# Block inverse of a gated-DeltaNet encoder: third 32x32 form in turn with the second, fifth 64x64 form in turn with the fourth of the next group

## The chip, the cores and the metric

The kernel runs on one core of one Trainium2 chip. The metric is device time of one execution in microseconds (us), lower is better. A core has a matrix engine (PE, TensorE, with weight loads listed apart as PEld), a vector engine (DVE), an activation engine (ACT), a general engine (POOL) and a queue engine for transfers (SP); each works through its own list of instructions in order, and they wait for each other by semaphores.

## What is computed

The reference is a two-layer encoder: in each layer a combined projection feeds a bidirectional chunked gated-delta-rule group (4 heads of 128) and a short gated convolution, then an output projection, then a SwiGLU feed-forward. The part that matters here is the triangular solve within each chunk, cut to its core:

```python
M = jnp.where(strict, jnp.einsum('bnhid,bnhjd->bnhij', kb, k) * decay_mat, 0.0)
A = M + jnp.eye(CHUNK, dtype=M.dtype)
u = lax.linalg.triangular_solve(A, vb, left_side=True, lower=True, unit_diagonal=True)
w = lax.linalg.triangular_solve(A, kb * jnp.exp(G)[..., None], left_side=True, lower=True,
                                unit_diagonal=True)
```

Instead of solving, the kernel forms the inverse of A once for each chunk, head and direction and multiplies by it in the scan over chunks. It uses chunks of 128 positions and a first chunk of 16.

## The kernel before

Data lie with channels on the 128 partitions and positions along the free dimension. A layer runs: input projection (function `dense`, lines 157 to 159, three matrix products for each part of the contraction, because each operand is split into a high and a low part), convolutions and gates, the chunk matrices and their inverses, the scan (`scan_step`), the output projection and the feed-forward. The dense products are TensorE's steady stream; all the rest is placed between them. After each stretch of a dense product has been recorded, `dense` takes one function from each of the lists `jobs`, `jobs2` and `jobs3` and calls it. `low(f)` records the matrix products of `f` at the place in the priority order that the dense products have reached, so that the scheduler, which orders the instructions of each engine by priority and by its own estimate of when they are ready, puts them among the dense ones.

The inverse of a 128x128 unit triangular block is built from its diagonal 32x32 blocks up. There are 32 such blocks (8 chunks x 4 heads) for each direction `d` in each layer, so four inverses in all. First DVE inverts the 32x32 diagonal blocks by substitution (`substitute`, lines 523 and 525), two 32x32-transposes (lines 534 and 535) give them in both orientations, and ACT writes one of them into the big matrix `P_` (line 537). Then `invert(d)` returns seven functions, which `jobs3` hands out one at a time:

- `first` (line 550): for each of 32 blocks q and two pairs (f, s) of neighbouring 32-strips, the product of the off-diagonal block with one diagonal inverse. ACT moves it to `QS` with its sign changed (line 553).
- `second` (line 558): `QS` of strip s times the other inverse, for the two pairs in turn; ACT moves it into `P_` (line 561). This gives the 64x64 inverses.
- `third` (line 568): the same product transposed, for the first pair only; ACT moves it into `X64` (line 569), and DVE fills the rest of `X64` with copies and zeros (lines 570 to 572).
- `fourth(qh)` and `fifth(qh)` (lines 579 and 584): the two 64x64 products that join the 64x64 inverses into 128x128 ones, for a group of eight blocks (qh 0 to 3). The fourth reads partitions F_ and writes partitions S_, the fifth reads S_ and writes F_ (F_ and S_ are the two halves of 64 partitions, which half is which depends on `d`). ACT moves the fourth's result into `X64` (line 580), which is the fifth's operand, and the fifth's into `P_` (line 585).

Each form takes PSUM from `fb(c)`, one bank of 128 partitions x 512 words; there are two banks for each direction ("f" for d = 0, "b" for d = 1). The first three forms take one bank for each half of 16 blocks, the last two one for each group of eight. A form that has been handed out in one job is followed by some 17 to 24 dense or other products before the next. The last four jobs are two groups of the fourth, two of the fifth, and once more:

```python
return [first, second, third] + [lambda f=f, q=q: [f(q), f(q + 1)] for q in (0, 2) for f in (fourth, fifth)]
```

[...]

Of the kernel before, what the change touches and what calls it, by code (L numbers as in the profile page):

```python
# [10 lines left out]
AF = mybir.ActivationFunctionType  # L11
# [31 lines left out]
def trunk(ctx: ExitStack, tc: tile.TileContext, xT, w_in, w_ba, w_out, w_gu, w_dn,  # L43
          par_d, alog_d, dtb_d, cst_d, eye_d, out):
    nc = tc.nc
# [10 lines left out]
    def big(tag, dt=F32):  # L56
        return sb.tile([128, 4, L], dt, tag=tag, name=nm(tag))
# [10 lines left out]
    def bank(tag):  # L68
        return psp.tile([128, 512], F32, tag=tag, bufs={"acc": 3, "a": 1, "f": 2, "b": 2}[tag], name=nm("p" + tag))
# [4 lines left out]
    turn = [0]  # L74
# [20 lines left out]
    def at_prio(p):  # L95
        tc.cur_priority = p

    mm = nc.tensor.matmul
    act = nc.scalar.activation
# [180 lines left out]
    for l in range(DEPTH):  # L280
# [213 lines left out]
        B = [slice(32 * b, 32 * b + 32) for b in range(4)]  # L494
# [32 lines left out]
        def invert(d):  # L527
            P_ = Pv[d]
            W, Xi = subs[d]
            tmp = tmp0[0] if d == 0 else big(Y[0][2])  # L530
            XB = tmp[:, 3, 0:1024].rearrange("p (q c) -> p q c", q=32)

            ZB = W.rearrange("p a b -> p (a b)").rearrange("p (q i) -> p q i", q=32)
            nc.vector.transpose(out=XB.rearrange("p q c -> p c q"), in_=Xi.rearrange("p i c -> p c i"))
            nc.vector.transpose(out=ZB.rearrange("p q i -> p i q"), in_=Xi)
            for b in range(4):
                act(out=P_[B[b], :, B[b]], in_=ZB[B[b]], func=AF.Copy)
            pairs = [(0, 1), (2, 3)] if d == 0 else [(3, 2), (1, 0)]
            QS = tmp[:, 2, 0:1024].rearrange("p (q c) -> p q c", q=32)
            X64 = tmp[:, 0:2, :].rearrange("p a b -> p (a b)")[:, 0:2048].rearrange("p (q c) -> p q c", q=32)  # L540
            halves = [slice(0, 16), slice(16, 32)]

            def fb(c):
                return bank("fb"[d]).rearrange("p (q c) -> p q c", c=c)


            def first():
                for qs in halves:
                    ps = fb(32)
                    low(lambda: [mm(ps[B[s], q - qs.start, :], P_[B[f], q, B[s]], XB[B[f], q, :], start=True, stop=True, skip_group_check=True)  # L550
                                 for q in range(qs.start, qs.stop) for (f, s) in pairs])
                    for (f, s) in pairs:
                        act(out=QS[B[s], qs, :], in_=ps[B[s]], func=AF.Copy, scale=-1.0)

            def second():
                for qs in halves:
                    ps = fb(32)
                    low(lambda: [mm(ps[B[f], q - qs.start, :], QS[B[s], q, :], P_[B[s], q, B[s]], start=True, stop=True, skip_group_check=True)
                                 for q in range(qs.start, qs.stop) for (f, s) in pairs])
                    for (f, s) in pairs:  # L560
                        act(out=P_[B[f], qs, B[s]], in_=ps[B[f]], func=AF.Copy)

            def third():
                f, s = pairs[0]
                fo, so = 32 * (f % 2), 32 * (s % 2)
                for qs in halves:
                    ps = fb(32)
                    low(lambda: [mm(ps[B[s], q - qs.start, :], P_[B[s], q, B[s]], QS[B[s], q, :], start=True, stop=True) for q in range(qs.start, qs.stop)])
                    act(out=X64[B[s], qs, fo:fo + 32], in_=ps[B[s]], func=AF.Copy)
                    nc.vector.tensor_copy(X64[B[f], qs, fo:fo + 32], XB[B[f], qs, :])  # L570
                    nc.vector.tensor_copy(X64[B[s], qs, so:so + 32], XB[B[s], qs, :])
                    nc.vector.memset(X64[B[f], qs, so:so + 32], 0.0)


            F_, S_ = (slice(0, 64), slice(64, 128)) if d == 0 else (slice(64, 128), slice(0, 64))

            def fourth(qh):
                ps = fb(64)
                low(lambda: [mm(ps[S_, q, :], P_[F_, 8 * qh + q, S_], X64[F_, 8 * qh + q, :], start=True, stop=True) for q in range(8)])
                act(out=X64[S_, 8 * qh:8 * qh + 8, :], in_=ps[S_], func=AF.Copy, scale=-1.0)  # L580

            def fifth(qh):
                ps = fb(64)
                low(lambda: [mm(ps[F_, q, :], X64[S_, 8 * qh + q, :], P_[S_, 8 * qh + q, S_], start=True, stop=True) for q in range(8)])
                act(out=P_[F_, 8 * qh:8 * qh + 8, S_], in_=ps[F_], func=AF.Copy)

            return [first, second, third] + [lambda f=f, q=q: [f(q), f(q + 1)] for q in (0, 2) for f in (fourth, fifth)]

        l2s = {}

# [84 lines left out]
        def low(f):  # L675

            here = tc.cur_priority
            at_prio(mmp[0])
            f()
            mmp[0] = tc.cur_priority  # L680
            at_prio(here)
# [21 lines left out]
        for i in range(4):  # L703
            t = trow()
            if i == 3:
                jobs3.extend(invert(0))
            inproj(8 + i, to_row(t))
            v = trow() if i % 2 == 0 else row(Y[1] + "f")
            conv(t, v, P_CV + 3 * (8 + i))
            act(out=v, in_=v, func=AF.Silu)  # L710
            jobs.extend([lambda i=i, v=v, c0=c0: v_store(i, v, c0) for c0 in (0, 1, 5)])
# [25 lines left out]
        for j, q in enumerate((4, 5, 0, 6, 7, 1, 2, 3)):  # L737
            lov[0] = j < 2
            if j == 1:
                jobs2.extend([lambda c=c: chunk_a(c) for c in ca])  # L740
            if j == 3:
                jobs3.extend(invert(1))
            if q < 4:
                y3 = sc_tile(q)
            else:
                z_tile(q - 4)
            if j == 0:
                substitute(1)
# [531 lines left out]
        for f in range(FT):  # L1280
# [22 lines left out]
            ps = {}  # L1303
# [107 lines left out]
        for u, (p, b, m) in enumerate(UNITS):  # L1411
            if b == 1 and p in FIRST:
                dh, z = FIRST[p]
                q = 4 * dh + m
# [13 lines left out]
            for j in range(NJ):  # L1428
                ps = bks[m, j]
# [21 lines left out]
        else:  # L1451
# [22 lines left out]
            for (n0, n1) in FIN:  # L1474
                e = (n1 - n0) // 4
                sv = ss[:, n0:n1]
                ps = bank("a")
# [100 lines left out]
```

## Time and profile before

| | |
|---|---|
| median of 3 runs (lowest to highest) | 2513.88 us (2511.24 to 2517.37) |
| the profiled execution's own time | 2517.22 us |
| its span, first to last instruction | 2515.4 us |
| mean granted TensorE clock | 0.997 |
| DVE, ACT busy, share of the span | 67%, 42% |

The profile is one execution. Its span is what its views divide up; the 1.8 us between span and time lie before the first and behind the last instruction. A matrix product of 32-bit operands is two records in the trace, each with its own weight load, so counts of records are twice those of the code; the records overlap, since the next one starts before the last has drained, and so the start-to-start distance, not the length of a record, is what a product takes from the queue.

### The profile page before, as it was taken

To read this page: it belongs to the slowest core of one execution; us is meant where nothing else is said; L and a number is where in the kernel's file an instruction comes from. 1 tells how busy PE (TensorE), PEld (TensorE's weight loads), DVE (VectorE), ACT (ScalarE), POOL (GpSimd) and SP (SyncE) were. 2 spreads that over 40 slices of the span, in tenths; PEclk is the share of its full clock that TensorE was granted. 3 is DMA by queue.
4 is the path that set the end of the run, shared out by engine and by line. 5 is a ranking of instruction groups with operands and counts; after the bars stand their busy time and mean duration, and the time that the engine had idled before them with its cause. 6 is when DMAs were issued, how large, how long until landed. Compare 5 with 4: busy or idle time off the path is not lost. (4 is left out here: it accounts for less than half of the span.)

```text
span 2515.4 us, 44862 instructions
## 1 busy us (share of the span) xinstructions
PE 2478.2 (99%) x17508; PEld 2276.9 (91%) x17508; DVE 1696.9 (67%) x3073; ACT 1045.9 (42%) x1944; POOL 340.0 (14%) x359
## 2 busy tenths in 40 slices
PE   8999999999999999999999999999999999999998
PEld 6989999999999999999999888998977888887887
DVE  4788333649877777877657893336698777677765
ACT  5554333535333333344445543335453333234444
POOL 1031212331000000000111212133400000000012
PEclk9999999999999999999999999999999999999999
DMA  3444353624323332764224443446332233238541
GB/s 127 135 166 149 112 161 130 212 77 136 116 102 102 108 102 81 256 198 133 92 77 145 152 154 116 143 131 205 120 126 101 97 105 117 90 112 279 177 120 68
DMA packets 199530, 335.27 MB, mean 133 GB/s; under 512 B 23404, under 2 KB 85668, under 8 KB 199316
## 3 DMA queue, kind: packets, MB, share of 16 engines
q1 hardware_dynamic: 171204, 293.84, 35.3%
q10 hardware_dynamic: 25936, 34.19, 4.2%
q0 software_dynamic: 2176, 4.36, 0.6%
q8 instruction: 138, 2.26, 0.4%
q14 instruction: 76, 0.62, 0.1%
HBM read 250.31 MB, written 81.99 MB: 132 GB/s over the span
## 5 line engine op out<-in xcount | busy, mean ns | idle before, releaser
L131 POOL TENSOR_TENSOR wlo<-raw,whi 128x512 fp32r<-128x512 f32 x132 | 176.4, 1338 | 1285.4 <-ACT whi L130 1116.7
L157 PE MATMUL pacc<-a,whi 128*128 128x346 f32 (+1 forms) x808 | 263.6, 329 | 8.8 <-ACT whi L130 7.6
L159 PE MATMUL pacc<-a,wlo 128*128 128x346 f32 (+1 forms) x808 | 262.4, 326 | 0.7 <-DVE wlo L131 0.5
L157 PE MATMUL pacc<-b,whi 128*128 128x346 f32 (+2 forms) x672 | 234.0, 349 | 2.4 <-ACT b L900 1.8
L159 PE MATMUL pacc<-b,wlo 128*128 128x346 f32 (+2 forms) x672 | 233.1, 348 | 0.8 <-DVE wlo L131 0.8
L158 PE MATMUL pacc<-a,whi 128*128 128x346 f32 (+1 forms) x688 | 225.1, 327 | 0.0
L130 ACT ACTIVATE whi<-raw 128x512 fp32r<-128x512 f32 x168 | 106.0, 631 | 228.3 <-PE pacc L158 124.9
L158 PE MATMUL pacc<-b,whi 128*128 128x346 f32 (+2 forms) x580 | 200.8, 346 | 0.0
L157 PEld LDWEIGHTS pacc<-a,whi 128*128 128x128 f32 x808 | 152.2, 189 | 14.6 <-ACT whi L130 8.1
L159 PEld LDWEIGHTS pacc<-a,wlo 128*128 128x128 f32 x808 | 152.9, 189 | 1.7 <-DVE wlo L131 0.8
L157 PEld LDWEIGHTS pacc<-b,whi 128*128 128x128 f32 x672 | 126.9, 189 | 14.5 <-issue 3.1
L159 PEld LDWEIGHTS pacc<-b,wlo 128*128 128x128 f32 x672 | 126.6, 189 | 9.8 <-DVE wlo L131 1.1
L158 PEld LDWEIGHTS pacc<-a,whi 128*128 128x128 f32 x688 | 130.3, 189 | 2.6 <-issue 2.1
L997 ACT ACTIVATE whi<-rw 128x512 fp32r<-128x512 f32 x92 | 57.6, 631 | 140.1 <-PE pf L1016 36.4
L158 PEld LDWEIGHTS pacc<-b,whi 128*128 128x128 f32 x580 | 109.5, 189 | 6.9 <-issue 0.4
L997 ACT ACTIVATE b<-rw 128x512 fp32r<-128x512 f32 x64 | 39.9, 631 | 135.0 <-PE pacc L1016 37.4
L296 DVE TENSOR_TENSOR a<-pacc,rstd 128x346 f32<-128x346 f32 (+2 forms) x59 | 32.7, 555 | 89.6 <-PE pacc L159 89.5
L296 DVE TENSOR_TENSOR b<-pacc,rstd 128x346 f32<-128x346 f32 (+1 forms) x63 | 32.5, 516 | 82.8 <-PE pacc L159 82.8
L131 POOL TENSOR_TENSOR a<-raw,a 128x512 fp32r<-128x512 f32 x3 | 3.9, 1285 | 597.1 <-ACT a L130 597.1
L997 ACT ACTIVATE a<-rw 128x512 fp32r<-128x512 f32 x64 | 40.0, 629 | 101.7 <-PE pacc L1016 60.3
L998 DVE TENSOR_TENSOR wlo<-rw,whi 128x512 fp32r<-128x512 f32 x92 | 62.8, 686 | 4.8 <-ACT whi L997 4.1
L1015 PE MATMUL pacc<-b,whi 128*128 128x260 f32 (+1 forms) x172 | 53.5, 311 | 0.7 <-ACT b L1051 0.7
(966 smaller groups left out, 8012.8 us busy)
## 6 DMA issues: line engine op xcount, KB each, us to landing
raw<-in_w_in SPq DMA_DIRECT2D x112, 256.0 KB, 2.5
raw<-in_w_gu SPq DMA_DIRECT2D x104, 256.0 KB, 2.9
rw<-in_w_gu SPq DMA_DIRECT2D x88, 256.0 KB, 3.0
rw<-in_w_dn SPq DMA_DIRECT2D x94, 192.0 KB, 2.7
rec<-vkd SPq DMA_DIRECT2D x61, 256.0 KB, 2.7
raw<-in_w_out SPq DMA_DIRECT2D x48, 256.0 KB, 2.8
b<-ad SPq DMA_DIRECT2D x45, 260.0 KB, 3.3
a<-ad SPq DMA_DIRECT2D x45, 256.0 KB, 5.2
```

The costliest lines, as they stand in the source:

```text
L130: whi_done[0] = act(out=hi, in_=raw[:, 0:kk, :], func=AF.Copy)
L131: (tt if lov[0] else ptt)(out=lo, in0=raw[:, 0:kk, :], in1=hi.bitcast(F32), op=ALU.subtract)
L157: mm(ps[:, :n], wh, xh[:, n0:n1], start=(k == 0), stop=False)
L158: mm(ps[:, :n], wh, xl[:, n0:n1], start=False, stop=False)
L159: mm(ps[:, :n], wl, xh[:, n0:n1], start=False, stop=(k == K - 1))
L296: tt(out=t[:, n0:n1], in0=ps, in1=rstd[:, n0:n1], op=ALU.mult)
L997: act(out=hi, in_=src, func=AF.Copy)
L998: tt(out=lo, in0=src, in1=hi.bitcast(F32), op=ALU.subtract)
L1015: mm(ps[:, :CW], w[0][:, k, :], th[:, cs], start=first and k == 0, stop=False, skip_group_check=True)
```

## The change

`second` and `third` become one function, `second_third`: for each block q the second form's two products and the third's are issued one after the other into one bank, and the ACT copies of both follow. `fourth` and `fifth` become `fourth_fifth(q4, q5)`: for each of eight blocks a product of the fourth form for group q4 and one of the fifth form for group q5 are issued in turn, into the two halves of one bank. It is called with (0, none), (1, 0), (2, 1), (3, 2) and (none, 3). `invert` still returns seven functions, and the arithmetic of each product is the same.

```diff
-            def second():
+            def second_third():
+                f0, s0 = pairs[0]
+                fo, so = 32 * (f0 % 2), 32 * (s0 % 2)
                 for qs in halves:
                     ps = fb(32)
-                    low(lambda: [mm(ps[B[f], q - qs.start, :], QS[B[s], q, :], P_[B[s], q, B[s]], start=True, stop=True, skip_group_check=True)
-                                 for q in range(qs.start, qs.stop) for (f, s) in pairs])
+                    def turn(q):
+                        for (f, s) in pairs:
+                            mm(ps[B[f], q - qs.start, :], QS[B[s], q, :], P_[B[s], q, B[s]], start=True, stop=True, skip_group_check=True)
+                        mm(ps[B[s0], q - qs.start, :], P_[B[s0], q, B[s0]], QS[B[s0], q, :], start=True, stop=True, skip_group_check=True)
+                    low(lambda: [turn(q) for q in range(qs.start, qs.stop)])
                     for (f, s) in pairs:
                         act(out=P_[B[f], qs, B[s]], in_=ps[B[f]], func=AF.Copy)
-            def third():
-                f, s = pairs[0]
-                fo, so = 32 * (f % 2), 32 * (s % 2)
-                for qs in halves:
-                    ps = fb(32)
-                    low(lambda: [mm(ps[B[s], q - qs.start, :], P_[B[s], q, B[s]], QS[B[s], q, :], start=True, stop=True) for q in range(qs.start, qs.stop)])
-                    act(out=X64[B[s], qs, fo:fo + 32], in_=ps[B[s]], func=AF.Copy)
+                    act(out=X64[B[s0], qs, fo:fo + 32], in_=ps[B[s0]], func=AF.Copy)
...
-            def fourth(qh):
+            def fourth_fifth(q4, q5):
                 ps = fb(64)
-                low(lambda: [mm(ps[S_, q, :], P_[F_, 8 * qh + q, S_], X64[F_, 8 * qh + q, :], start=True, stop=True) for q in range(8)])
-                act(out=X64[S_, 8 * qh:8 * qh + 8, :], in_=ps[S_], func=AF.Copy, scale=-1.0)
-            def fifth(qh):
-                ps = fb(64)
-                low(lambda: [mm(ps[F_, q, :], X64[S_, 8 * qh + q, :], P_[S_, 8 * qh + q, S_], start=True, stop=True) for q in range(8)])
-                act(out=P_[F_, 8 * qh:8 * qh + 8, S_], in_=ps[F_], func=AF.Copy)
-            return [first, second, third] + [lambda f=f, q=q: [f(q), f(q + 1)] for q in (0, 2) for f in (fourth, fifth)]
+                def turn(q):
+                    if q4 is not None:
+                        mm(ps[S_, q, :], P_[F_, 8 * q4 + q, S_], X64[F_, 8 * q4 + q, :], start=True, stop=True, skip_group_check=True)
+                    if q5 is not None:
+                        mm(ps[F_, q, :], X64[S_, 8 * q5 + q, :], P_[S_, 8 * q5 + q, S_], start=True, stop=True, skip_group_check=True)
+                low(lambda: [turn(q) for q in range(8)])
+                if q4 is not None:
+                    act(out=X64[S_, 8 * q4:8 * q4 + 8, :], in_=ps[S_], func=AF.Copy, scale=-1.0)
+                if q5 is not None:
+                    act(out=P_[F_, 8 * q5:8 * q5 + 8, S_], in_=ps[F_], func=AF.Copy)
+            return [first, second_third] + [lambda a=a, b=b: fourth_fifth(a, b) for a, b in ((0, None), (1, 0), (2, 1), (3, 2), (None, 3))]
```

More of the change, by code (lines that the diff above doesn't have):

```diff
@@ L560, in second @@
                     for (f, s) in pairs:
                         act(out=P_[B[f], qs, B[s]], in_=ps[B[f]], func=AF.Copy)
-            def third():
-                f, s = pairs[0]
-                fo, so = 32 * (f % 2), 32 * (s % 2)
-                for qs in halves:
-                    ps = fb(32)
-                    low(lambda: [mm(ps[B[s], q - qs.start, :], P_[B[s], q, B[s]], QS[B[s], q, :], start=True, stop=True) for q in range(qs.start, qs.stop)])
-                    act(out=X64[B[s], qs, fo:fo + 32], in_=ps[B[s]], func=AF.Copy)
-                    nc.vector.tensor_copy(X64[B[f], qs, fo:fo + 32], XB[B[f], qs, :])
-                    nc.vector.tensor_copy(X64[B[s], qs, so:so + 32], XB[B[s], qs, :])
-                    nc.vector.memset(X64[B[f], qs, so:so + 32], 0.0)
+                    act(out=X64[B[s0], qs, fo:fo + 32], in_=ps[B[s0]], func=AF.Copy)
@@ L575, in invert @@
+                    nc.vector.tensor_copy(X64[B[f0], qs, fo:fo + 32], XB[B[f0], qs, :])
+                    nc.vector.tensor_copy(X64[B[s0], qs, so:so + 32], XB[B[s0], qs, :])
+                    nc.vector.memset(X64[B[f0], qs, so:so + 32], 0.0)
             F_, S_ = (slice(0, 64), slice(64, 128)) if d == 0 else (slice(64, 128), slice(0, 64))
-            def fourth(qh):
+            def fourth_fifth(q4, q5):
                 ps = fb(64)
-                low(lambda: [mm(ps[S_, q, :], P_[F_, 8 * qh + q, S_], X64[F_, 8 * qh + q, :], start=True, stop=True) for q in range(8)])
-                act(out=X64[S_, 8 * qh:8 * qh + 8, :], in_=ps[S_], func=AF.Copy, scale=-1.0)
```

## The prediction

> **What bounds the kernel now.** I read the page's head first, then busy time by stretch for the four places where the inverse is assembled (two layers, two directions), then TensorE's instructions in order of time there.
>
> ```profile
> span 2515.4 us, 44862 instructions
> ...
> PE 2478.2 (99%) x17508; PEld 2276.9 (91%) x17508; DVE 1696.9 (67%) x3073; ACT 1045.9 (42%) x1944; POOL 340.0 (14%) x359
> ```
>
> TensorE has work in 99% of the span, so the question is whether that also holds where the change sits. In the next rows the columns are the stretch, its length, then busy us and count for PE, its weight loads (PEld), DVE, ACT and POOL, the granted clock, the DMA share and GB/s.
>
> ```profile
> 205.00:250.00 45.00, 45.00 (x648) 43.12 (x647) 40.59 (x87) 24.10 (x35) 8.00 (x6) 1.00 0.56 181
> 275.00:325.00 50.00, 50.00 (x664) 47.84 (x663) 4.68 (x9) 16.37 (x26) 12.32 (x9) 1.00 0.27 90
> 1460.00:1505.00 45.00, 45.00 (x622) 40.42 (x621) 41.18 (x86) 23.67 (x35) 8.88 (x8) 1.00 0.55 177
> 1530.00:1585.00 55.00, 55.00 (x650) 48.21 (x648) 5.53 (x9) 16.85 (x27) 15.96 (x11) 1.00 0.24 84
> ```
>
> In all four, PE is busy for the whole stretch; no other engine is, though DVE comes near in the first and third (40.59 of 45, 41.18 of 45: the other direction's substitution). So these stretches are TensorE's queue, and an instruction taken off it moves everything behind it forward, as long as nothing behind it is late for another reason. But "busy" does not say that the array is full: here small products run one after another. That is read from the timeline (start, length, engine, line, operation, tile shape, shape, count). Second and third form of one inverse, with the dense products around them:
>
> ```profile
> 286.90 0.32 PE L159 MATMUL pacc<-a,wlo 128*128 128x346 f32 x1
> 287.16 2.21 PE L558 MATMUL pb<-P,b 32*32 32x32 f32 x128
> 289.30 0.42 PE L157 MATMUL pacc<-a,whi 128*128 128x346 f32 x1
> 289.56 0.32 PE L158 MATMUL pacc<-a,whi 128*128 128x346 f32 x1
> 289.72 0.32 PE L159 MATMUL pacc<-a,wlo 128*128 128x346 f32 x1
> ...
> 293.06 0.32 PE L159 MATMUL pacc<-a,wlo 128*128 128x346 f32 x1
> 293.31 2.21 PE L568 MATMUL pb<-b,P 32*32 32x32 f32 x64
> 295.45 0.42 PE L157 MATMUL pacc<-a,whi 128*128 128x348 f32 x1
> 295.71 0.32 PE L158 MATMUL pacc<-a,whi 128*128 128x348 f32 x1
> ```
>
> The reader should see that 128 records take 2.21 us and 64 records of the same size take 2.21 us too. (Each product of the program is two records.) The 128 are the second form: two pairs in turn, whose operands and results lie in different 32-partition strips. The 64 are the third form, all in one strip. So two strips in turn run side by side, and one strip alone runs at half that rate: 2.21/64 = 0.035 us a record, against 0.017.
>
> **The change part by part.** I price a block of small products by what it adds to the queue: from the start of the dense product before it to the start of the second one after it (the first one after is held up too), less two normal dense steps of 0.16 (289.56 to 289.72).
>
> Second form: 289.56 - 286.90 - 0.32 = 2.34. Third form: 295.71 - 293.06 - 0.32 = 2.33. The grouped view gives the mean length of one record behind the busy time:
>
> ```profile
> L568 PE MATMUL pb<-b,P 32*32 32x32 f32 x64 | 2.2, 191 | 0.0
> ```
>
> So 2.21 - 0.19 = 2.02 is 63 steps from start to start, 0.032 each; 64 of them are 2.05, and 0.28 of the 2.33 is entry and exit.
>
> *Third in turn with second.* The third form's products now stand between the second's, so its block as such is gone. The third uses the same operand strip as the second's first pair (partitions 32 to 63 or 64 to 95) but another result strip. No row shows three 32x32 strips in turn. Bounds: if the third fits beside the other two, as the second pair fits beside the first, it costs nothing and 2.33 is saved. If it must queue behind the pair whose operand strip it shares, that strip has 128 records at 0.032, 4.10 + 0.28 = 4.38 against 4.67 now: 0.29 saved. The nearest row is a sum over partitions, four products that share all 128 operand partitions and write four different result strips:
>
> ```profile
> 624.36 0.28 PE L1016 MATMUL pacc<-a,whi 128*128 128x260 f32 x1
> 624.47 0.28 PE L1017 MATMUL pacc<-a,wlo 128*128 128x260 f32 x1
> 624.68 0.65 PE L207 MATMUL pa<-rstd,ones 128*32 128x260 f32 x8
> 625.25 0.39 PE L1015 MATMUL pb<-P,a 128*128 128x260 f32 x1
> ```
>
> Eight records of 260 columns, and the next dense product starts 0.57 after the first of them; one after another, at even the 0.11 of a dense record of 260 columns (624.36 to 624.47), they would take 0.88. So products that share operand partitions do run side by side when their result strips differ. I take 2.33. [...]
>
> *Fifth in turn with fourth.* Fourth and fifth form now:
>
> ```profile
> 299.21 0.32 PE L159 MATMUL pacc<-a,wlo 128*128 128x348 f32 x1
> 299.46 2.07 PE L579 MATMUL pb<-b,P 64*64 64x64 f32 x32
> 301.47 0.43 PE L157 MATMUL pacc<-a,whi 128*128 128x346 f32 x1
> 301.74 0.31 PE L158 MATMUL pacc<-a,whi 128*128 128x346 f32 x1
> ...
> 305.22 0.32 PE L159 MATMUL pacc<-a,wlo 128*128 128x346 f32 x1
> 305.47 2.08 PE L584 MATMUL pb<-P,b 64*64 64x64 f32 x32
> 307.48 0.43 PE L157 MATMUL pacc<-a,whi 128*128 128x346 f32 x1
> ```
>
> A block of 32 records costs 301.74 - 299.21 - 0.32 = 2.21, and the fifth the same (both 2.26 to the first dense start). Two groups of the fourth, then two of the fifth, twice: 4 x 2.21 = 8.84 an inverse. In one place of layer 2 the block is cut in halves, which gives the price of a record:
>
> ```profile
> 1483.19 1.14 PE L579 MATMUL pf<-a,P 64*64 64x64 f32 x16
> 1484.26 0.44 PE L698 MATMUL pa<-ident,a3f 128*128 128x128 f32 x2
> ```
>
> Sixteen last 1.14, thirty-two 2.07: 0.93/16 = 0.058 a record. Of the 2.21, then, 32 x 0.058 = 1.86 is records and 0.35 is entry and exit. The new form has five blocks of one bank: fourth alone, three mixed, fifth alone. A mixed block has 16 records of either kind; fourth reads the F half and writes the S half, fifth the reverse, so both strips differ, as with the two pairs of the second form. If they run side by side, each block is 16 steps: 16 x 0.058 + 0.35 = 1.28, and five are 6.40: 2.44 saved. The other bound, nothing side by side: three blocks of 2.21 and two of 1.28, 9.19: 0.35 lost. The nearest row, the second form with 128 records in 2.21, is exactly this case at 32 wide; I take 2.44. [...]
>
> *What the order of instructions makes of it.* In the changed program fourth and fifth do stand strictly in turn, and second and third as written. In three of the four inverses one product of the fourth form is put ahead of its block, alone: 2 x 0.058 + 0.35 = 0.47 each, 1.41. The cut block of layer 2 is whole now: 0.35 back. The engines have as many instructions as before, DMAs too (SP, ACT and POOL queues keep theirs, some a few places earlier or later).
>
> *Evacuations.* As many ACT copies as before, but a half of the second form now releases three together, and each mixed block two. What is queued behind is the next block, which waits on TensorE for them, with all dense work behind it.
>
> ```profile
> 288.40 2.40 ACT L561 ACTIVATE P<-pb 32x512 f32<-32x512 f32 x4 [3.74 <-PE pb L558]
> ...
> 229.82 1.07 ACT L670 ACTIVATE b<-b 128x1040 f32<-128x1040 f32 x1
> ```
>
> Copies take 2.40/4 = 0.60. The first half's begin while the block still runs (288.40, block's end 289.3). The fourth's first groups need the first half only: three copies, done by 288.40 + 1.80 = 290.2, where 18 to 24 other products (2.9 to 3.8 us) cover until 292.2 at least. From one mixed block to the next stand 20 other products or more, 3.2 us at 0.16, over two copies (1.2) and one long ACT operation ahead (1.07): 0.9 to spare. I cost these waits at nothing; cover gone, each waits what ACT is late. The second direction's inverse also starts earlier, by what the first one saves; its inputs have room:
>
> ```profile
> 251.87 0.19 DVE L525 TENSOR_TENSOR x<-x,Tm 128x31 f32<-128x31 f32 x1
> ...
> 279.10 0.31 PE L550 MATMUL pb<-b,P 32*32 32x32 f32 x8
> ```
>
> Substitution ends at 252, the first form starts at 279.
>
> *Sum.* 4 x (2.33 + 2.44) = 19.1, less 1.41, plus 0.35: 18.0 us. The profiled execution took 2517.2 (span 2515.4 and 1.8 around it), so 2499.2; that execution is 3.3 above the median 2513.9 of three runs (2511.2 to 2517.4), so on the median's scale 2495.9, say 2496. Behind the inverse, scan steps move by up to 28 dense products against the dense stream. There TensorE does wait today:
>
> ```profile
> 480.00:495.00 15.00, 13.67 (x100) 12.98 (x99) 11.48 (x29) 12.75 (x44) 3.77 (x3) 1.00 0.80 299
> 1728.00:1740.00 12.00, 9.95 (x47) 8.12 (x46) 9.03 (x14) 8.86 (x27) 4.19 (x3) 0.86 0.98 362
> ```
>
> 1.33 and 2.05 idle, 3.4 together: it can go, or double; 3.4 either way.
>
> **The rivals.**
> A. *Third queues behind the second's first pair* (shared operand strip): 0.29 for 2.33, four times, 8.2 less: 9.8 saved, 2504. For: no row has 32x32 strips sharing operands. Against: the four-strip sum. 10%.
> B. *The 64x64 halves do not overlap*: 2.44 becomes -0.35, 11.2 less: 6.8 saved, 2507. For: no 64x64 pair in the trace. Against: the second form. 7%.
> C. *The change does not do what it says*, neither overlaps: 4 x (0.29 - 0.35) - 1.06 = -1.3, about 2515. Needs both. 3%.
> D. *Slower: the block start becomes the wait.* Place: 16 starts that wait for the copies of the block before (after the first of five, four in each inverse). Price: what ACT is late beyond the cover of 3.2. At 18/16 = 1.1 us each the saving is gone; from 1.4 (18 + 5, over 16) it is slower beyond noise; three more long operations ahead of the copies, 3 x 1.07 less the 0.9 to spare, give 2.3 each, 37: 2533. For: DVE and ACT are loaded in the first and third stretch. Against: ACT is busy 16 of 50 us in the second and 17 of 55 in the fourth. 5%.
>
> **How the numbers follow.** Forecast 75%: 2496, of itself 2489 to 2503 (3.4 of scan waits and 3 of spread between runs). Up to A and B the range ends at 2507; below, 2488, since no more idle is there to win: the tails hold C, D and half of B. 0.2% is 5 us, about what a measurement of this kernel tells from no change. Faster: forecast, A and 5 of B's 7, 0.90; same: C and the rest of B, 0.05; slower: D, 0.05.
>
> **What would show it.** Right: one block of 192 records at 32x32 in about 2.2 us; mixed 64x64 blocks of 32 records in about 1.14, with no L568-like block left; PE busy still the whole stretch; some 4.5 us less per inverse. A shows as 192 records in about 4.2, B as mixed blocks at 2.07, D as idle PE before mixed blocks with ACT as releaser. A loss or gain above 4 us in the scan stretches would make the prediction wrong though the blocks are right.

## The result, and the profile after

| | before | after |
|---|---|---|
| median (lowest to highest), 6 runs each on one chip | 2514.10 us (2511.24 to 2518.01) | 2501.30 us (2498.91 to 2505.99) |
| profiled execution, its span | 2517.22, 2515.4 us | 2502.22, 2500.1 us |
| mean granted TensorE clock | 0.997 | 0.997 |

The ratio after to before is 0.9944, 95% interval 0.9934 to 0.9954: 12.8 us between the medians, 15.0 between the two profiled executions, where 18.0 were forecast. The head of the page and the four stretches of the inverse, in the columns of before:

```profile
span 2500.1 us, 44874 instructions
...
PE 2461.5 (98%) x17508; PEld 2257.4 (90%) x17508; DVE 1693.0 (68%) x3073; ACT 1045.0 (42%) x1944; POOL 339.3 (14%) x359
```

```profile
205.00:250.00 45.00, 43.45 (x648) 40.88 (x647) 39.67 (x91) 22.42 (x34) 8.46 (x6) 0.92 0.56 187
275.00:325.00 50.00, 50.00 (x693) 46.99 (x693) 5.19 (x10) 18.95 (x35) 13.38 (x11) 1.00 0.33 111
1460.00:1505.00 45.00, 44.39 (x580) 40.64 (x574) 42.67 (x86) 18.92 (x30) 9.91 (x7) 1.00 0.59 192
1530.00:1585.00 55.00, 54.95 (x617) 48.32 (x611) 5.56 (x12) 19.89 (x37) 13.62 (x10) 1.00 0.30 99
```

The work has moved forward by up to 12 us under these fixed windows, so their counts cannot be compared. Busy time and clock can: the second and fourth stretch are full, but the first has lost 1.55 us of PE and its clock is 0.92, where before had 45.00 and 1.00; the third has lost 0.61.

First the blocks that went right. The timeline of after around the merged second and third form of the second inverse, then its records and those of one mixed 64x64 block, grouped (count, busy us, mean ns):

```profile
285.74 0.32 PE L159 MATMUL pacc<-a,wlo 128*128 128x346 f32 x1
285.99 0.22 PE L563 MATMUL pb<-P,b 32*32 32x32 f32 x2
286.00 0.21 PE L564 MATMUL pb<-b,P 32*32 32x32 f32 x1
...
288.02 0.19 PE L564 MATMUL pb<-b,P 32*32 32x32 f32 x1
288.14 0.42 PE L157 MATMUL pacc<-a,whi 128*128 128x346 f32 x1
288.40 0.32 PE L158 MATMUL pacc<-a,whi 128*128 128x346 f32 x1
```

```profile
L563 PE MATMUL pb<-P,b 32*32 32x32 f32 x128 | 2.2, 191 | 0.0
L564 PE MATMUL pb<-b,P 32*32 32x32 f32 x64 | 2.2, 191 | 0.0
```

```profile
L585 PE MATMUL pb<-P,b 64*64 64x64 f32 x16 | 1.1, 221 | 0.0
L583 PE MATMUL pb<-b,P 64*64 64x64 f32 x16 | 1.1, 221 | 0.0
```

The 64 records of the third form lie inside the 2.2 us of the 128 of the second. The block's price, worked out as in the prediction, is 288.40 - 285.74 - 0.32 = 2.34: what the second form alone cost. The mixed block and its neighbours:

```profile
302.55 0.32 PE L159 MATMUL pacc<-a,wlo 128*128 128x346 f32 x1
302.80 0.27 PE L583 MATMUL pb<-b,P 64*64 64x64 f32 x1
...
303.88 0.43 PE L157 MATMUL pacc<-a,whi 128*128 128x346 f32 x1
304.14 0.32 PE L158 MATMUL pacc<-a,whi 128*128 128x346 f32 x1
```

Its price is 304.14 - 302.55 - 0.32 = 1.27, against the 1.28 forecast. Now the block that went wrong, the merged one of the first inverse: its timeline in the middle, and its records as a group (last column: idle before, and what ended it):

```profile
216.40 0.19 PE L564 MATMUL pf<-b,P 32*32 32x32 f32 x1
218.14 0.26 PE L563 MATMUL pf<-P,b 32*32 32x32 f32 x2 [1.55 <-issue]
```

```profile
L563 PE MATMUL pf<-P,b 32*32 32x32 f32 x128 | 2.6, 197 | 1.5 <-issue 1.5
```

Between two records that elsewhere in the block start some 0.02 apart lie 1.74 us, and the releaser is "issue": no semaphore and no engine that the profile shows ended it. Towards its end the clock is halved (0.50). Two rows of after, the stretch behind the stall and the merged block of the third inverse, which has no such gap:

```profile
217.50:224.30 6.80, 6.16 (x47) 5.72 (x47) 5.77 (x16) 3.21 (x6) 0.00 (x0) 0.50 0.26 79
1466.40:1468.90 2.50, 2.50 (x195) 2.31 (x195) 2.33 (x6) 1.50 (x3) 1.32 (x1) 1.00 0.12 35
```

The half clock of 6.80 us begins while TensorE still stands (0.64 us); over the 6.16 busy us it takes 3.1 us of full-speed work. With the stall that is 4.8 us, more than one inverse saves.

Where the 15.3 us of span went is read from the start of the same dense product in both traces (counted in order), differences after less before. A small product that moves past a dense one counts in the neighbouring row:

| from, to (us in the kernel before) | what lies there | change |
|---|---|---|
| 0 to 205.2 | before the first inverse | -1.8 |
| 205.2 to 272.9 | first inverse (layer 1, d = 0) | +0.6 |
| 272.9 to 328.9 | second inverse (layer 1, d = 1) | -4.3 |
| 328.9 to 1455.1 | scan and rest of layer 1 | 0.0 |
| 1455.1 to 1515.9 | third inverse (layer 2, d = 0) | -3.9 |
| 1515.9 to 1532.6 | behind it | +2.0 |
| 1532.6 to 1584.1 | fourth inverse (layer 2, d = 1) | -4.4 |
| 1584.1 to 1749.9 | most of the scan of layer 2 | -2.4 |
| 1749.9 to 2479.9 | the scan's end (at 1796), then the rest of layer 2 | -1.1 |

The +2.0 is a new wait. The timeline of after there, and DVE's share in the window (DVE is the third pair of numbers):

```profile
1507.32 0.32 PE L159 MATMUL pacc<-b,wlo 128*128 128x346 f32 x1
1508.98 1.13 PE L485 MATMUL pb<-a,a 128*128 128x128 f32 x8 [1.34 <-DVE dt L489]
```

```profile
1500.00:1510.00 10.00, 8.66 (x60) 8.40 (x59) 9.65 (x14) 4.22 (x4) 0.00 (x0) 1.00 0.51 166
```

TensorE is earlier than before, DVE (9.65 of 10) is not, and the product of line 485 waits for it. In the scan of layer 2 it is the other way round. The timeline of before, its clock behind that wait, and the window of after that answers to the prediction's 1728 to 1740:

```profile
1731.77 1.06 PE L828 MATMUL pf<-vv,rec 128*128 128x128 f32 x8
1734.62 0.50 PE L157 MATMUL pacc<-b,whi 128*128 128x512 f32 x1 [1.80 <-ACT b L900]
```

```profile
1735.30:1738.70 3.40, 3.33 (x10) 2.87 (x11) 3.40 (x6) 3.40 (x9) 0.00 (x0) 0.51 1.01 410
```

```profile
1728.00:1740.00 12.00, 12.00 (x60) 9.86 (x59) 7.22 (x15) 2.82 (x9) 3.88 (x3) 1.00 0.72 257
```

The wait of 1.80 and the halved clock behind it are gone after the change.

### The profile page after: what moved, and what is told of

It reads as the page before. It is cut to its first block, busy times and chain, and to the rows that moved or that the text cites. A ratio compares the mean times of both kernels' runs of the same rounds, so it can differ in the third digit from the quotient of the medians.

```text
span 2500.1 us, 44874 instructions
## 1 busy us (share of the span) xinstructions
PE 2461.5 (98%) x17508; PEld 2257.4 (90%) x17508; DVE 1693.0 (68%) x3073; ACT 1045.0 (42%) x1944; POOL 339.3 (14%) x359
```

## The experiments

The stall needed a cause. "Issue" and a place inside a block whose operands are all there point at the instructions themselves. The page has 17508 weight loads beside 17508 products, so the merged block is 2 x 192 = 384 instructions in 2.03 us (285.99 to 288.02); before, 256 stood in the same time. The page also counts the packets that bring instructions:

```profile
q8 instruction: 137, 2.24, 0.4%
```

137 packets of 16 KB (138 in before); 2 x 17508 loads and products with 266 semaphore and drain instructions of TensorE are 137.8 times 256. By these counts TensorE's stream comes in pieces of 256 instructions. In the trace one such packet starts at 215.65 and ends at 216.53, and TensorE, which had 142 instructions left when it started (0.75 us at the block's pace), goes on at 218.14, 2.5 us after. Counted over the trace, 3265 = 12 x 256 + 193 of TensorE's instructions (loads, products and semaphore instructions) stand ahead of the stall; "before instruction 3265" means this count. That TensorE has then used up one piece and stands until the next is there is an estimate from these times (the fetch theory, F). If it holds, stalls sit at 256k + 193 and move with the number of instructions ahead of them. The rivals: a stall of the data or the bank of this block would stay with the block, and disturbance from outside would not come back.

**The changed kernel again** (on the chip of the next three).

> The changed kernel once more, as the partner of the other runs on this chip. Theory F (fetch): TensorE's instructions arrive in pieces of 16 KB, 256 instructions (the page's instruction queue; 138 packets, 2.26 MB); a piece is asked for when the one before it is begun and is usable some 3 us later; in the first inverse of layer 1 a whole piece lies inside the block of 192 records (384 instructions in 2.03 us), so TensorE runs dry for 1.7 us at the same place again, and the granted clock is halved for 6.8 us behind it. Theory W (wait): TensorE waited there for an ACT copy or a transfer that happened to be late; then the gap varies in place and length, or is absent. Time by both 2499 to 2504.

Measured: 2505.10 us (2499.37 to 2507.52) against 2517.12 (10 runs), ratio 0.9949 (0.9935 to 0.9963). The timeline:

```profile
220.18 0.22 PE L563 MATMUL pf<-P,b 32*32 32x32 f32 x2 [2.54 <-issue]
```

The stall came back before the same instruction 3265, longer (2.73 us from start to start), with 3.4 us of half clock behind it (0.50 in 220.50 to 223.90). It belongs to the program.

**The halves of the merged block apart**, the first group of the fourth form between them, so that 192 instructions stand together and not 384. The line with `after` holds the second half back until that group has been issued.

```diff
+                            if q == 16 and s == s0:
+                                after(ins, fourth0[0])
...
-            return [first, second_third] + [lambda ... for a, b in ((0, None), (1, 0), (2, 1), (3, 2), (None, 3))]
+            return [first, lambda: second_third(halves[:1]), lambda: fourth_fifth(0, None), lambda: second_third(halves[1:])] + [lambda ... for a, b in ((1, 0), (2, 1), (3, 2), (None, 3))]
```

> The two halves of the merged second and third form are handed out apart, with the first group of the fourth form between them, so that no piece of 256 instructions lies wholly inside blocks of small 32x32 products. Same products. Theory F: no gap over 1 us inside any block of the four inverses, no half clock around 215 to 226 us; 1.7 and half of 6.8 us come back, two more block entries of 0.3 us are paid: 4 to 5 us less than the changed kernel, 2496 to 2498. Theory W: the gap stays in the first inverse (the copies are as late as before), time within 1.5 us of the changed kernel or up to 1 us more.

Measured: 2508.15 us (2504.08 to 2513.79), ratio 0.9968 (0.9954 to 0.9981). Missed: 2496 to 2498 were expected. The stall and the half clock between 205 and 330 us are gone, and yet the kernel is no faster than the changed one. The new order makes waits of its own, read from the timeline (idle before, releaser):

```profile
235.52 0.27 PE L589 MATMUL pf<-P,b 64*64 64x64 f32 x1 [0.51 <-ACT b L593]
238.02 0.66 PE L708 MATMUL pa<-ident,b3f 128*128 128x128 f32 x4 [1.36 <-ACT b3f L709]
```

These two are not where most of it went. Counted as in the table above, the kernel gains 5.6 us from 205 to 320, where the changed kernel gains 3.7; but from 320 to 530, over the scan of layer 1, it loses 4.2 where the changed kernel gains 0.8. What makes the scan slower was not tried. So splitting cures the stall and isn't free. It can't tell by itself whether F is the cause, since it changed the order too.

**16 tiny products ahead of everything** (64 instructions), whose result nobody uses; the rest is the changed kernel. Only the borders of the pieces move.

```diff
     nc.vector.memset(ones, 1.0)
+    pad = bank("a")
+    for _ in range(16):
+        mm(pad[0:32, 0:16], ones[:, 0:32], ones[:, 0:16], start=True, stop=True, skip_group_check=True)
```

> The changed kernel with 16 tiny products (64 instructions) on TensorE at its start, while it waits for the first load: nothing else differs, but every later instruction stands 64 places further in its piece. Piece borders then fall at instruction 18 and 274 of the merged block in layer 1 direction 0, 172 in direction 1, 93 and 349 in layer 2 direction 0, 79 and 335 in direction 1. Theory F: gaps of 1 to 1.8 us inside three blocks (all but layer 1 direction 1), where the changed kernel has one; each costs 1.7 us, and up to 3.4 more where the clock is halved behind it: 2504 to 2512. Theory W: one gap at most, as before, time within 2 us of the changed kernel.

Measured: 2501.93 us (2497.36 to 2506.90), ratio 0.9933 (0.9916 to 0.9950). The timeline, one row from each of three inverses:

```profile
215.44 0.18 PE L567 MATMUL pf<-b,P 32*32 32x32 f32 x1 [0.32 <-issue]
...
1466.86 0.26 PE L566 MATMUL pf<-P,a 32*32 32x32 f32 x2 [2.19 <-issue]
...
1541.43 0.25 PE L567 MATMUL pb<-a,P 32*32 32x32 f32 x1 [2.00 <-issue]
```

The stall of the first inverse shrinks to 0.32 us idle, still before instruction 3265, and two blocks of layer 2 that had none stall for 2.2 and 2.0, before instructions 23745 and 25281, which are 92 x 256 + 193 and 98 x 256 + 193. Around the one of 2.2 the clock is 0.50 from 1465.60 to 1472.40, and the mean clock of the execution is 0.994, against 0.997 in after. The layer-1 inverses save 3.7 and 4.2 us here, the third one loses 0.3 in place of saving 3.9, and the fourth saves nothing. The places are those that F names, the lengths are not (1 to 1.8 us were expected). The median lies below the 2504 to 2512 expected; the profiled execution, 2506.90, is the slowest of the four.

**48 tiny products** (192 instructions), the same edit with another number.

> As the run before with 48 tiny products (192 instructions). Borders then fall at instruction 146 and 402 of the merged block in layer 1 direction 0, 44 and 300 in direction 1, 221 in layer 2 direction 0 and 207 in direction 1. Theory F: the gap in layer 1 direction 0 is gone, and one of 1 to 1.8 us appears in direction 1; a smaller one, under 1.2 us, may appear at the end of the first form in layer 2 direction 1, where 256 instructions lie in 2.0 us. Theory W: the gap stays in direction 0. Time 2499 to 2505 by both, so the place of the gap decides.

Measured: 2497.16 us (2496.68 to 2497.92), ratio 0.9920 (0.9907 to 0.9934). The timeline:

```profile
219.27 0.32 PE L162 MATMUL pacc<-a,wlo 128*128 128x346 f32 x1 [1.49 <-issue]
...
286.30 0.18 PE L567 MATMUL pb<-b,P 32*32 32x32 f32 x1 [2.03 <-issue]
```

Now the second inverse stalls (before instruction 5057 = 19 x 256 + 193), and in the first the stall is 17 instructions behind the block, in the dense stream (3521 = 13 x 256 + 193). None is left in the blocks of layer 2. With 0, 16 and 48 products every such stall lies at 256k + 193, in whichever inverse that border falls. Counted over all twelve traces, the second of two borders inside one merged block stalls every time (eight blocks), and a block with a single border never does. That settles the cause: not the block's data, but where the piece ends.

**46 tiny products, and the two halves of the second form handed out as two jobs in d = 1 only**, so that no whole piece lies inside one block.

```diff
+    for _ in range(46):
+        mm(pad[0:32, 0:16], ones[:, 0:32], ones[:, 0:16], start=True, stop=True, skip_group_check=True)
...
-            return [first, second_third] + [...]
+            return [first] + [lambda h=h: second_third(h) for h in ([halves] if d == 0 else [halves[:1], halves[1:]])] + [...]
```

> The changed kernel with 46 tiny products (184 instructions) at its start and, for direction 1 alone, the two halves of the merged form in two jobs. Piece borders then fall at instruction 154 and 410 of the whole block in layer 1 direction 0 and at 232 in layer 2 direction 0; in direction 1 the halves are 192 instructions each with 24 dense products between. No piece of 256 lies inside a block. Theory F: no gap over 1 us in or right behind a merged block, no half clock from 205 to 330 and from 1455 to 1590 us that follows such a gap; the first inverse saves 4.3 us like the others; 4 to 6 us less than the changed kernel on the same chip (ratio to the kernel before 0.991 to 0.9935). Theory W (the gap is a wait for ACT or a transfer): as the changed kernel, ratio 0.994 to 0.996.

Measured: 2502.22 us (2500.91 to 2503.47) against 2516.54 (23 runs, the chip of this and the next three), ratio 0.9943 (0.9930 to 0.9955). A ratio of 0.991 to 0.9935 was expected: missed. No merged block stalls inside; just behind the first one, where the next border lies, 1.16 us pass from start to start (the profile puts the wait down to a DVE line). From 205 to 1455 us the kernel gains 7.2 by the count of the table, where the changed kernel gains 3.7; from 1455 to 1800 it gains 2.7, where the changed kernel gains 9.3. What was won in layer 1 was lost to a larger wait in layer 2 (4.39 us, and a half clock of 3.4 behind it), from the timeline, and what DVE did meanwhile (1470.9 to 1475.5, grouped):

```profile
1475.53 0.78 PE L707 MATMUL pa<-ident,a3f 128*128 128x128 f32 x4 [4.39 <-DVE vm L700]
```

```profile
L526 DVE TENSOR_TENSOR Tm<-x,x 128x255 f32<-128x255 f32 (+3 forms) x5 | 2.1, 421 | 0.1
L528 DVE TENSOR_TENSOR x<-x,Tm 128x255 f32<-128x255 f32 (+3 forms) x5 | 2.1, 418 | 0.1
...
L700 DVE COPY vm<-pa 16x128 f32<-16x128 f32 x1 | 0.3, 272 | 0.0
```

The small copy that TensorE wants (0.3 us) stands behind ten operations of the other direction's substitution (4.2 us). Clear borders were worth about as much as this one wait cost.

**Third in turn with second alone**; fourth and fifth as before.

```diff
...
-            return [first, second_third] + [lambda a=a, b=b: fourth_fifth(a, b) for ...]
+            return [first, second_third] + [lambda f=f, q=q: [f(q), f(q + 1)] for q in (0, 2) for f in (fourth, fifth)]
```

> Only the third form in turn with the second; fourth and fifth as in the kernel before. By the prediction's term 4 x 2.33 = 9.3 us less. Theory F: one merged block (layer 1 direction 0, borders at 82 and 338) runs dry, 1.7 to 2.7 us and up to 3.4 of half clock behind it: 9.3 less 2 to 6, so 3 to 7 us less than before, ratio 0.997 to 0.9988. Theory W: the same with the gap anywhere or nowhere, 7 to 9.5 less. In the trace 192 records in 2.0 to 2.1 us in the three other inverses by both.

Measured: 2517.98 us (2514.86 to 2520.36), ratio 1.0003 (0.9994 to 1.0012): nothing gained, a clear miss. The first inverse stalls before instruction 3265 again (1.27 us idle). More is lost in the scan of layer 1 and behind it: by the count of the table the kernel is 1.5 us ahead of before at 320, 7.3 behind at 530 and 11.8 behind at 610, having waited 2.69 us for ACT just before. A window of the scan in before, and the same in this kernel with one row of its timeline:

```profile
489.00:504.00 15.00, 14.69 (x108) 14.45 (x107) 12.03 (x31) 9.15 (x31) 8.31 (x10) 1.00 0.87 330
```

```profile
489.00:504.00 15.00, 10.92 (x45) 9.07 (x44) 14.49 (x17) 7.99 (x23) 15.00 (x15) 0.67 0.86 324
```

```profile
491.86 0.42 PE L158 MATMUL pacc<-a,whi 128*128 128x348 f32 x1 [0.99 <-DVE a L901]
```

PE is busy for 10.92 us where it was for 14.69, waiting for DVE while DVE (14.49) and POOL (15.00) are full, and the clock is 0.67. Of what the merged block saves in layer 1 nothing arrives. Between 1455 and 1836 us in before's time, over layer 2's inverses and its scan, the kernel gains 4.9, and two blocks at 2.33 are 4.7; but at 1584, behind both inverses, it has lost 0.8, so this agreement may be chance.

**Fifth in turn with fourth alone**; second and third as before.

```diff
...
-            return [first, second, third] + [lambda f=f, q=q: [f(q), f(q + 1)] for q in (0, 2) for f in (fourth, fifth)]
+            return [first, second, third] + [lambda a=a, b=b: fourth_fifth(a, b) for a, b in ((0, None), (1, 0), (2, 1), (3, 2), (None, 3))]
```

> Only the fifth form in turn with the fourth of the next group; second and third as in the kernel before. By the prediction's term 4 x 2.44 = 9.8 less, 1.4 for three single products and 0.35 back: 8.7 us less. No small block holds a whole piece of 256 instructions, so theory F sees no gap: 7.5 to 10 less than before, ratio 0.996 to 0.997, and so more than the third form alone brings. If the two merges were alike but for their terms (no running dry), this one brings as much as the third form alone, within 1 us.

Measured: 2507.02 us (2502.08 to 2511.07), ratio 0.9959 (0.9945 to 0.9974), 9.5 between the medians; the prediction's terms for this part are 4 x 2.44 - 1.41 + 0.35 = 8.7. No block stalls. The stretch of the first inverse:

```profile
205.00:250.00 45.00, 45.00 (x664) 42.96 (x664) 42.93 (x94) 23.41 (x35) 10.35 (x7) 1.00 0.62 204
```

PE is full and the clock whole, where the changed kernel had 43.45 and 0.92. By the count of the table the trace leads before's by 8.7 at 2479.9, of which 5.9 were won between 205 and 1800 us, over the inverses and scans; so the nearness of 9.5 to 8.7 is in part chance.

**The kernel before with 46 tiny products**, to see what pads do without the change.

```diff
+    for _ in range(46):
+        mm(pad[0:32, 0:16], ones[:, 0:32], ones[:, 0:16], start=True, stop=True, skip_group_check=True)
```

> The kernel before with the same 46 tiny products at its start: what the padding itself does. Both theories: no block of 192 records, so no running dry; time within 2.5 us of the kernel before. If the padding alone (a warmer start, another place of the pieces in the rest of the kernel) brings more than 4 us, the gain of the run with clear borders isn't due to the borders in the inverse.

Measured: 2511.17 us (2509.25 to 2513.84), ratio 0.9977 (0.9968 to 0.9986): 5.4 us faster, where at most 2.5 were expected, and none of it in an inverse (the lead over before is 2.07 us from 205 to 329 us, unchanged). So a padded kernel must be compared with a padded one: the run with clear borders is 8.9 us faster than this one, and not 14.3.

**48 products in both kernels**, on one chip: the kernel before, then the changed one.

> The kernel before with 48 tiny products (192 instructions of TensorE) at its start whose result nobody uses; all else as before. Theory P (the pads themselves bring what the run with 46 of them showed, 5.4 us, at the start and in the late wait near 2300 us): 2509 to 2512, ratio 0.997 to 0.9985, and not the inverse. Theory N (the pads bring nothing, the 5.4 us were scatter of one chip): 2513 to 2518, ratio 0.999 to 1.001.

> The changed kernel with the same 48 products at its start, once more, on the same chip. Theory F (what is left behind the change is instruction fetch, half clock and the late wait): 2497 to 2500 as in the first run, ratio to the kernel before 0.9915 to 0.9935. Against the kernel before with the same pads the change alone then is worth 12 to 14 us (P) or 17 to 19 us (N). If the first run was scatter, it lies at 2501 to 2505 like the changed kernel without pads.

Measured: before 2518.83 us (15 runs); before with pads 2513.47 (2508.76 to 2514.80, 11 runs), ratio 0.9978 (0.9969 to 0.9986); changed with pads 2496.59 (2494.25 to 2497.03, 5 runs), ratio 0.9912 (0.9898 to 0.9926). The pads alone bring 5.4 us again, the change with pads 16.9; 12 to 14 were expected if the pads did so. Between the two padded traces the changed one leads by 15.9 us at 2479.9: 12.0 were won from 205 to 1800 us, where the change acts, 2.7 before the first inverse and 1.2 behind. The pair without pads has 13.0 in that same stretch. So by these two pairs of traces the change itself is worth 12 to 13 us, and not 18. Of the 4.9 by which the padded kernel before leads at 2479.9, 2.7 are a late wait in the last feed-forward with the half clock behind it (0.50 in 2312.20 to 2315.60 of before; 1.00 in 2308.50 to 2311.90 of before with pads). Its row in before, in before with pads, and in changed with pads:

```profile
2310.78 0.50 PE L1435 MATMUL pf<-P,a 128*128 128x512 f32 x1 [3.60 <-ACT a L1196]
```

```profile
2307.38 0.50 PE L1438 MATMUL pf<-P,a 128*128 128x512 f32 x1 [2.42 <-ACT a L1199]
```

```profile
2291.49 0.50 PE L1444 MATMUL pf<-P,a 128*128 128x512 f32 x1 [1.68 <-ACT a L1205]
```

Why an ACT result 2300 us later comes earlier is open; nothing was run on it. The changed kernel with 48 pads is the fastest version seen, in two sets of runs, but not a clean one: its second inverse still stalls, and part of its lead is that late wait.

## Why the prediction was right, and where its sum was off

*That TensorE's queue sets the end there* held: in the second and fourth inverse PE is busy throughout (50.00 of 50, 54.95 of 55), and most of what was taken off it arrived, 4.3 and 4.4 us. The sum for an inverse with a lone product is 2.33 + 2.44 - 0.47 = 4.30, as in the second; the fourth has none, so 4.77 were forecast there.

*Third in turn costs nothing* was right (2.34 for the merged block, as for the second form alone). Rival A, which would have shown 192 records in 4.2 us, is refuted by the 2.2 us of the block; products that share an operand strip run side by side here when their result strips differ.

*Fifth in turn with fourth* was right: 1.27 for a mixed block against 1.28. Rival B would have shown 2.07. Both being refuted, C falls too, while the total of the run with the fifth form alone, 9.5 us for terms of 8.7, says less, as shown there.

*The lone products*: forecast 0.47. Two records of line 583 stood alone at 297.24 between dense products; here is that stretch of the timeline of after:

```profile
296.99 0.32 PE L159 MATMUL pacc<-a,wlo 128*128 128x348 f32 x1
297.24 0.33 PE L583 MATMUL pb<-b,P 64*64 64x64 f32 x2
297.50 0.43 PE L157 MATMUL pacc<-a,whi 128*128 128x346 f32 x1
297.76 0.33 PE L158 MATMUL pacc<-a,whi 128*128 128x346 f32 x1
```

297.76 - 296.99 - 0.32 = 0.45.

*Block starts wait for nothing* (rival D) held nearly everywhere. The one visible case is in the third inverse, from the timeline of after:

```profile
1487.77 0.32 PE L157 MATMUL pacc<-b,whi 128*128 128x346 f32 x1
1488.70 0.27 PE L585 MATMUL pf<-P,a 64*64 64x64 f32 x1 [0.61 <-ACT a L589]
```

It starts 0.93 after the dense product, where 0.25 is normal (302.55 to 302.80): 0.7 lost, far from the 18 that D needed. With 48 pads another block start of the same inverse idles longer, so the cover that ACT has there is thin:

```profile
1492.73 1.14 PE L588 MATMUL pf<-P,a 64*64 64x64 f32 x16 [1.84 <-ACT a L592]
```

*The scan may move by 3.4 either way*: it moved by -2.9 in layer 2 (2.4, and 0.5 up to its end at 1796) and by some -0.8 in layer 1 (329 to 530). That this bound held is partly luck: in another order, with the third form alone, the same stretch of layer 1 lost 5.3.

*What the sum left out* is in the first inverse. "Costs nothing" was argued from strips and records alone, and the sum had no term for bringing instructions to TensorE. Merging raised the pace from 256 to 384 instructions in some 2 us. At that pace a piece of 256 that lies wholly in the block is used up in 1.35 us (256/384 of 2.03), and in after the next instruction ran only 2.5 us after its packet had begun (215.65 to 218.14). Priced by the profile of after: 1.7 of stall and 3.1 of half clock, 4.8 us. That is the shortfall of this inverse: 4.3 were forecast as saved, 0.6 was lost. Waits costed at nothing, or not in the sum at all, were the second step that failed: the ACT wait took 0.7 in the third inverse (3.9 saved for 4.30 + 0.35), and behind it the table has 2.0, of which the DVE wait shown explains 1.4 (1508.98 - 1507.32, less a normal 0.25). Together that is 7.5, and the four inverses and what follows them measure +0.6 - 4.3 - 3.9 + 2.0 - 4.4 = -10.0, against -18.0 forecast. The terms close within 0.5, 0.4 of it in the fourth inverse; the 2.0 is itself read from the table. The other 5.3 of the 15.3 came from elsewhere: 2.9 from the scan of layer 2, 1.8 before the first inverse and 0.6 behind. The last two are places that the change doesn't touch. The changed kernel's second trace has 0.8 in place of 1.8 before the first inverse, so that part is scatter between executions at least by half; a single profiled pair isn't good for 1 us. So it was partly luck that the time landed within the range: gains elsewhere made up for a loss that was not foreseen.

That the stall sits where a piece ends is shown by the moved borders (eight blocks, always at 256k + 193); that the next piece comes too late is concluded from that and from the one packet timed above. That the half clock is its consequence is seen as a sequence (from start to start: 0.50 for 6.8 us at the stalls of 1.7 us in after and 2.4 us with 16 tiny products; for 3.4 us behind that of 2.7 us in the changed kernel run again and that of 2.4 us in the second run with 48), not tried apart. Why the waits on DVE, ACT and POOL come and go with the order is argued from the rows of each trace only; what made DVE and POOL late in the scan of layer 1, with the third form alone, stays open.

## What to carry to other kernels

Here small products on disjoint result strips, issued in turn, added nothing to the queue, though they share operand rows (2.34 with the third form and without it); price such a merge by the nearest pair that already runs in turn. Then ask what the higher pace needs: count the instructions of the denser block, and where more than 256 of them stand together without dense work between, look for a stall. Here two borders fell into a block of 384 instructions eight times, and each time TensorE stood for 0.5 to 2.7 us; in after the clock went to 0.50 for 6.8 us with it. And before a padded or reordered kernel is credited with a gain, pad or reorder the kernel before in the same way: here that alone was worth 5.4 us.

## What the hardware showed that was not expected

TensorE stalled for 0.5 to 2.7 us (start to start) inside a block with all operands ready, in six traces, always with 256k + 193 of its instructions ahead (loads, products and semaphore instructions). In the profile of after the next instruction ran 2.5 us after the last packet before it began (215.65 to 218.14). In the dense stream 256 instructions last 20 us (two every 0.16 us), and no border there shows such a stall (in after the longest distance from start to start at one is 0.44 us); only directly behind a block of small products did one appear (17 instructions behind, 1.8 us, with 48 tiny products).

With a stall of only 1.7 us the granted clock fell to 0.50 for 6.8 us. Behind the 2.7 us of the changed kernel run again it was 0.50 for 3.4 us, and around the 2.4 us (1464.48 to 1466.86) in the third inverse with 16 tiny products for 6.8, so in these traces the price of a stall inside a block varies between 1.7 and 3.1 us of work beyond its own length. Length alone does not decide it: in the kernel before, TensorE's idle 1.80 us before 1734.62 was followed by a clock of 0.51 and its 1.73 us before 605.64 was not (1.00 in 605.64 to 609.04); nor were the 2.42 us before 2307.38 in the kernel before with 48 tiny products (1.00 in 2308.50 to 2311.90).
